# Four heads to a unit for short key ranges, and output projections in halves, in two attentions of a two-block transformer kernel

## The chip, the cores and the metric

One core of a Trainium2 chip runs the whole program. The metric is device time in microseconds (us), the median over several executions. The times of the kernel before are 1931.8, 1932.94 and 1935.67 us, median 1932.94. The engines are called PE (TensorE, matrix products; PEld is its loading of weights), DVE (VectorE), ACT (ScalarE), POOL (GpSimd) and SP (SyncE, which only issues DMAs here).

## What is computed

The reference runs two models after each other on 512 tokens of width 1024, four layers in all, in float32. The change touches the attention of the third and fourth layer only (`fox_attention` with `memory_attention`, and `dilated_attention` with `memory_attention`). Cut to that:

```
h = x                                    # [512, 1024]
for layer in (0, 1):
    xn = rmsnorm(h, norm_mix[layer])
    q, k, v, (f,) qm = split(xn @ w_in)  # 12 heads of 64 for q, k, v; 4 memory heads qm
    if layer == 0:                       # fox: causal, with a forget term per head and key
        sc = q @ k.T / 8 + c[query] - c[key]
    else:                                # dilated: causal, each key weighted by how many
        sc = q @ k.T / 8 + log(count)    # of three dilated windows hold it
    mix = softmax(sc) @ v                # 12 heads, up to 512 keys
    mem_out = softmax(qm @ km.T / 8) @ vm   # 4 heads, 256 memory keys
    h = h + concat(mix, mem_out) @ w_out[layer]
    h = h + conv_ffn(rmsnorm(h, norm_ffn[layer]))
```

(The reference computes the dilated attention as three branches joined by their log-sum-exps; over 512 tokens that is the softmax above, and the kernel uses it in that form.)

## The kernel before

Both attentions come from `attn34` (line 1214), once with `li == 0` (fox) and once with `li == 1` (dilated). It first projects q, k, v and prepares the memory keys, which the change leaves alone. The part that is touched begins at line 1346.

Queries are worked in four blocks of 128 (`qb`), in the order 3, 2, 0, 1. Block `qb` sees `128 * (qb + 1)` keys, so block 3 has 512 and block 0 has 128; the memory heads have 256 keys always. A *unit* is two heads (`j`, 0 to 5 mixing heads, 6 and 7 memory heads) of one query block: 32 units. The loop at line 1424 is a pipeline of three parts on PE. Step `i` issues, in this order:

- **S**, `score` of unit `i` (line 1350): the two heads' products q·k into two PSUM banks, one head in each, and in the fox attention's mixing heads two more matmuls for the forget term. On DVE and ACT the softmax follows: per head one DVE pass that adds the mask and takes the row extreme (line 1372; for memory heads a plain reduction, 1376), one ACT exponential with its sum (1377), then one DVE reciprocal for both heads (1380), and one DVE scaling per head (1382).
- **V**, `value` of unit `i - 2` (line 1396): the products with v, into the bank `o`. After every fourth `j`, `group` (1409) splits the bank into a high part on ACT (`ah`) and a low part on DVE (`al`).
- **T**, `turn_p` of unit `i - 1` (line 1384): transposes of the two heads' probabilities, one PSUM bank a head, each copied out by `evac`, two on ACT to one on DVE.
- whatever is due by `steps.tick()` (1444).

Every S, V and T matmul, and those of the output projection, go through `Chain`, so PE takes them in the order in which they were written. `Steps` holds work to be issued some ticks later. When all eight pairs of a query block are done, `group` books `finish` three ticks later (1417). `finish` (836) does the output projection in four quarters of 256 columns, 24 matmuls each, one quarter a tick (`per=1`), in the bank `misc`, of which there is one; two quarters fill it, and DVE then adds it to `h` (859). After the last quarter come the next layer's norm (`norm_scale`, 237) and, four ticks later, `to_x` (260): eight transposes in two portions that go through `misc` too, each copied out by ACT (268) and DVE (269). These transposes are not in the chain: where they stand in PE's order is set when the program is planned. The last block (`qb` 1) uses `o` for its second half and puts its `to_x` off into the next phase. `finish` is shared with the first layer's attention (882 to 968), which already works with four heads to a unit in the same two score banks and with halves (`per=2`), and two ticks between.

The banks: one `o`, one `misc`, two pairs of score banks `spp`, two `tps` for transposes. The probabilities have four buffers (`p2`), the transposed ones two (`pt`).

Of the kernel before, what the change touches and what calls it, by code (L numbers as in the profile page):

```python
# [8 lines left out]
F32 = mybir.dt.float32  # L9
F32R = mybir.dt.float32r  # L10
BF = mybir.dt.bfloat16
AF = mybir.ActivationFunctionType
OP = mybir.AluOpType
AX = mybir.AxisListType
# [83 lines left out]
def _build(tc, nc, ctx, t, out, dbg, upto):  # L98
    V, A, G, PE = nc.vector, nc.scalar, nc.gpsimd, nc.tensor
# [10 lines left out]
    nrm = pool(ctx, "nrm", 1)  # L110
# [14 lines left out]
    def pst(tag):  # L125
        return banks[tag].tile([128, 512], F32, tag=tag, name=tag)
# [228 lines left out]
    def evac(dst, src):  # L355
        evq[0] += 1
        if evq[0] % 3 == 0:
            V.tensor_copy(dst, src)
        else:
            A.activation(dst, src, AF.Copy)  # L360
# [19 lines left out]
    pp = phase(pst_, "prep", side="right")  # L380
# [6 lines left out]
    qT = l1.tile([128, 4, 512], F32, name="qT")  # L387
    kT = l1.tile([128, 2, 512], F32, name="kT")
    vt = l1.tile([128, 4, 128], F32, name="vt")
# [36 lines left out]
    for tb in range(NB):  # L426
# [7 lines left out]
        tp = pst("ft")  # L434
# [26 lines left out]
    pt = pp.tile([128, 3, 16], F32, name="pt")  # L461
# [288 lines left out]
    steps = Steps()  # L750
# [85 lines left out]
    def finish(steps, ws, cat, tb, gb, x, last, pl, chain=None, per=1):  # L836
        def norm():
            if last:
                norm_block(h[:, tb], gb, x, tb, pl=pl, put_off=pend.append)
            else:  # L840
                norm_block(h[:, tb], gb, x, tb, ("misc", "misc"), pl, lambda f: steps.later(4, f))

        tags = ("misc", "o") if last else ("misc", "misc")
        if chain is None:
            out_proj(ws, cat, tb, tags)
            norm()
            return
        bank = {}

        def quarter(c):  # L850

            half, q = divmod(c, 2)
            if q == 0:
                bank["ps"] = pst(tags[half])
            ps = bank["ps"]
            tm(ps[:, q * 256:(q + 1) * 256], ws[c], cat, pe=chain)
            if q == 1:
                hv = h[:, tb, half * 512:(half + 1) * 512]
                V.tensor_tensor(hv, ps, hv, op=OP.add)
            if c == 3:  # L860
                norm()
            elif (c + 1) % per:
                quarter(c + 1)
            else:
                steps.later(1, lambda: quarter(c + 1))
        quarter(0)
# [11 lines left out]
    steps = Steps()  # L878
    chain = Chain()
# [74 lines left out]
    units = [(qb, kv) for qb in range(NB - 1, -1, -1) for kv in range(2)]  # L954
    sts = {qb: {} for qb in range(NB)}
    for i in range(len(units) + 2):
        if i < len(units):
            qb, kv = units[i]
# [3 lines left out]
        if i > 1:  # L962
            qb, kv = units[i - 2]
# [3 lines left out]
        if 0 < i <= len(units):  # L967
            qb, kv = units[i - 1]
# [14 lines left out]
    qT = l2.tile([128, 8, 512], F32, name="qT2")  # L983
    kT = l2.tile([128, 2, 512], F32, name="kT2")
    vt = l2.tile([128, 4, 256], F32, name="vt2")
# [17 lines left out]
    steps = Steps()  # L1003
# [39 lines left out]
    tp = tps()  # L1043
    for tb in range(NB):
        PE.transpose(tp[:, tb * 8:tb * 8 + 8], wiT[64:72, tb * 128:(tb + 1) * 128], ident[64:72, 64:72])
    V.tensor_scalar(wi.rearrange("p b h -> p (b h)"), tp[:, :32], float(np.float32(8 ** -0.5)), 0.125,
                    op0=OP.mult, op1=OP.mult)
# [9 lines left out]
    for qb in range(1, NB):  # L1057
        n = 128 * (qb + 1)
        qs = slice(qb * 128, qb * 128 + 128)
        s_ = ix.tile([128, 512], F32, tag=f"isc{qb}", name="isc")[:, :n]  # L1060
        for hd in range(8):
            rw = slice((hd % 2) * 64, (hd % 2) * 64 + 64)
# [151 lines left out]
    def attn34(li, x3, w_in, w_out_ap, gain_next):  # L1214
# [132 lines left out]
        steps = Steps()  # L1347
        chain = Chain()

        def score(qb, j, st_):  # L1350
            qs = slice(qb * 128, qb * 128 + 128)
            nm, sm = st_["nm"], st_["sm"]
            m = 128 * (qb + 1) if j < 6 else 256
            rows = [slice(i * 64, i * 64 + 64) for i in range(2)]
            forget = li == 0 and j < 6
            pp = spp()
            for i, rw in enumerate(rows):
                if j < 6:
                    chain.matmul(pp[:, i, :m], qT[rw, j, qs], kT[rw, j, :m], start=True, stop=not forget)
                else:  # L1360
                    chain.matmul(pp[:, i, :m], qmT[rw, j - 6, qs], kmT[rw, j - 6], start=True, stop=True)
            if forget:
                for i in range(2):
                    chain.matmul(pp[:, i, :m], sel[rows[i], 2 * j + i:2 * j + i + 1].to_broadcast([64, 128]),
                                 c24[rows[i], :m], start=False, stop=True)
            h2 = slice(2 * j, 2 * j + 2)
            for i in range(2):
                hd = 2 * j + i
                p2 = ae.tile([128, 512], F32, tag="p2", name="p2", bufs=4)
                src = pp[:, i]  # L1370
                if j < 6:
                    V.tensor_tensor_reduce(out=p2[:, :m], in0=src[:, :m], in1=nlm[:, 512 - m:], scale=1.0,
                                           scalar=3e38, op0=OP.add, op1=OP.min, accum_out=nm[:, hd:hd + 1])
                    src = p2
                else:
                    V.tensor_reduce(nm[:, hd:hd + 1], src[:, :m], axis=AX.X, op=OP.min)
                A.activation(p2[:, :m], src[:, :m], AF.Exp, bias=nm[:, hd:hd + 1], scale=-1.0,
                             accum_out=sm[:, hd:hd + 1])
                st_[hd] = p2
            V.reciprocal(sm[:, h2], sm[:, h2])  # L1380
            for hd in (2 * j, 2 * j + 1):
                V.tensor_scalar(st_[hd][:, :m], st_[hd][:, :m], sm[:, hd:hd + 1], None, op0=OP.mult)

        def turn_p(qb, j, st_):
            m = 128 * (qb + 1) if j < 6 else 256
            st_["pt", j] = []
            for i in range(2):
                p2 = st_[2 * j + i]
                tp = tps()
                for kb in range(m // 128):  # L1390
                    chain.transpose(tp[:, kb * 128:(kb + 1) * 128], p2[:, kb * 128:(kb + 1) * 128], ident)
                pt_ = ae.tile([128, 512], F32, tag="pt", name="pt_", bufs=2)
                evac(pt_[:, :m], tp[:, :m])
                st_["pt", j].append(pt_)

        def value(qb, j, st_):
            m = 128 * (qb + 1) if j < 6 else 256
            jj = j % 4
            if jj == 0:
                st_["po", j // 4] = pst("o")  # L1400
            pov = st_["po", j // 4].rearrange("p (j q) -> p j q", j=4)
            for kb in range(m // 128):
                for i in range(2):
                    hd = 2 * j + i
                    vv = vt[:, kb, hd * 64:(hd + 1) * 64] if j < 6 else vm[:, kb, (hd - 12) * 64:(hd - 11) * 64]
                    chain.matmul(pov[i * 64:(i + 1) * 64, jj], vv, st_["pt", j][i][:, kb * 128:(kb + 1) * 128],
                                 start=kb == 0, stop=kb == m // 128 - 1)

        def group(qb, hg, st_):
            po = st_["po", hg]  # L1410
            ah = ap_.tile([128, 4, 128], F32R, tag="ah", name="ah", bufs=3)
            al = ap_.tile([128, 4, 128], F32R, tag="al", name="al", bufs=3)
            A.activation(f3(ah), po, AF.Copy)
            V.tensor_tensor(f3(al), po, f3(ah).bitcast(F32), op=OP.subtract)
            st_["a", hg] = (ah, al)
            if hg == 1:
                steps.later(3, lambda: finish(
                    steps, wo, lambda k: (st_["a", k // 4][0][:, k % 4], st_["a", k // 4][1][:, k % 4]), qb, gb, xn_,
                    qb == order[-1], ap_ if order.index(qb) % 2 else nrm, chain))

        order = (3, 2, 0, 1)
        units = [(qb, j) for qb in order for j in range(8)]
        sts = {qb: {} for qb in range(NB)}
        for i in range(len(units) + 2):
            if i in (1, 2):
                q = int(i == 2)
                ps = pst("misc")
                fm(ps, w, q * 128, 128, xk(x3))
                A.activation(qmT[:, q], ps, AF.Copy, scale=-0.125)
            if i < len(units):  # L1430
                qb, j = units[i]
                if j == 0:
                    sts[qb]["nm"] = ae.tile([128, 16], F32, tag="nm", name="nm", bufs=2)
                    sts[qb]["sm"] = ae.tile([128, 16], F32, tag="sm", name="sm", bufs=2)
                score(qb, j, sts[qb])
            if i > 1:
                qb, j = units[i - 2]
                value(qb, j, sts[qb])
                if j % 4 == 3:
                    group(qb, j // 4, sts[qb])  # L1440
            if 0 < i <= len(units):
                qb, j = units[i - 1]
                turn_p(qb, j, sts[qb])
            steps.tick()
        steps.drain()
        stx.close()
# [163 lines left out]
```

## Time and profile before

| | us |
|---|---|
| median of 3 runs | 1932.94 |
| the profiled execution, whole | 1937.1 |
| its span, first to last instruction | 1935.2 |
| PE busy | 1833.9 (95%) |
| DVE busy | 1039.4 (54%) |
| ACT busy | 728.6 (38%) |
| stretch of the fox attention from its first memory unit to the last projection | 117.7 |
| the same stretch of the dilated attention | 118.1 |

Busy times come from one execution recorded by the hardware profiler. A matmul's recorded end is modelled and matmuls overlap, so a busy PE need not be a PE at its peak; the granted clock (PEclk, 1.00 is 2.4 GHz and 0.50 is 1.2 GHz) stands beside it. The chain of waits is followed backwards from the last instruction, and each entry is what the end of the program was waiting for at that moment.

### The profile page before, as it was taken

To read this page: it belongs to the slowest core of one execution; us is meant where nothing else is said; L and a number is where in the kernel's file an instruction comes from. 1 tells how busy PE (TensorE), PEld (TensorE's weight loads), DVE (VectorE), ACT (ScalarE), POOL (GpSimd) and SP (SyncE) were. 2 spreads that over 40 slices of the span, in tenths; PEclk is the share of its full clock that TensorE was granted. 3 is DMA by queue.
4 is the path that set the end of the run, shared out by engine and by line. 5 is a ranking of instruction groups with operands and counts; after the bars stand their busy time and mean duration, and the time that the engine had idled before them with its cause. 6 is when DMAs were issued, how large, how long until landed. Compare 5 with 4: busy or idle time off the path is not lost.

```text
span 1935.2 us, 27920 instructions
## 1 busy us (share of the span) xinstructions
PE 1833.9 (95%) x11098; PEld 1540.4 (80%) x11100; DVE 1039.4 (54%) x2199; ACT 728.6 (38%) x1454; POOL 132.9 (7%) x151
## 2 busy tenths in 40 slices
PE   6999969999999999999999999999989899999998
PEld 5987759859789887678888888889957788888886
DVE  5874474268664534664655553366275555555522
ACT  4133353333443334543443341233264444333421
POOL 1332001203120000000000000000000000000000
PEclk9999989969999999989999999999999999999999
DMA  6112321301521432102333322333220043322321
GB/s 207 44 34 88 131 66 51 98 22 56 166 72 41 149 109 77 33 1 66 110 100 88 101 74 98 110 130 98 78 87 1 3 120 98 99 87 82 115 87 66
DMA packets 187898, 161.74 MB, mean 84 GB/s; under 512 B 14568, under 2 KB 170320, under 8 KB 187768
## 3 DMA queue, kind: packets, MB, share of 16 engines
q1 hardware_dynamic: 181168, 144.30, 24.1%
q0 software_dynamic: 2784, 9.00, 1.5%
q10 hardware_dynamic: 3816, 6.66, 1.0%
q8 instruction: 88, 1.44, 0.3%
q14 instruction: 42, 0.34, 0.1%
HBM read 157.88 MB, written 4.74 MB: 84 GB/s over the span
## 4 chain that ended last, share of the span: by engine, by line
PE 81%; DVE 7%; issue 4%; DMA 3%; ACT 3%; POOL 1%; ACTq 0%; POOLq 0%; DVEq 0%; SPq 0%
PE acc L212 19%; PE acc L210 19%; PE acc L211 19%; PE misc L338 6%; PE o L338 3%; PE tps L338 2%; PE spp L338 2%; DVE wl L206 1%; PE sps L1064 1%; PE misc L210 1%; PE misc L211 1%; PE misc L212 1%; PE o L1140 1%; ACT wh L204 1%; DVE xn L247 1%
## 5 line engine op out<-in xcount | busy, mean ns | idle before, releaser
L206 DVE TENSOR_TENSOR wl<-raw,wh 128x1024 fp32r<-128x1024 f32 (+3 forms) x250 | 299.1, 1207 | 408.2 <-ACT wh L204 407.3
L204 ACT ACTIVATE wh<-raw 128x1024 fp32r<-128x1024 f32 (+2 forms) x262 | 270.3, 1044 | 475.6 <-PE acc L211 208.9
L212 PE MATMUL acc<-xh,wl 128*128 128x512 f32 (+2 forms) x1032 | 391.0, 380 | 4.3 <-DVE wl L206 4.3
L210 PE MATMUL acc<-xh,wh 128*128 128x512 f32 (+2 forms) x1032 | 391.6, 381 | 0.7 <-ACT xh L268 0.5
L211 PE MATMUL acc<-xl,wh 128*128 128x512 f32 (+2 forms) x1032 | 391.0, 380 | 0.0
L212 PEld LDWEIGHTS acc<-xh,wl 128*128 128x128 f32 (+1 forms) x1032 | 193.9, 188 | 45.0 <-DVE wl L206 5.9
L210 PE MATMUL acc<-wh,xh 128*128 128x256 f32 (+1 forms) x736 | 224.5, 305 | 3.0 <-ACT xh L268 2.8
L210 PEld LDWEIGHTS acc<-xh,wh 128*128 128x128 f32 (+1 forms) x1032 | 193.1, 188 | 40.7 <-ACT xh L268 1.0
L211 PEld LDWEIGHTS acc<-xl,wh 128*128 128x128 f32 (+1 forms) x1032 | 193.8, 188 | 38.0
L211 PE MATMUL acc<-wl,xh 128*128 128x256 f32 (+1 forms) x736 | 220.6, 300 | 1.1 <-DVE wl L206 1.1
L212 PE MATMUL acc<-wh,xl 128*128 128x256 f32 (+1 forms) x736 | 220.2, 300 | 0.8 <-DVE xl L269 0.8
L210 PEld LDWEIGHTS acc<-wh,xh 128*128 128x128 f32 x736 | 152.5, 207 | 10.1 <-ACT xh L268 5.8
L212 PEld LDWEIGHTS acc<-wh,xl 128*128 128x128 f32 x736 | 152.7, 208 | 6.0 <-issue 4.3
L211 PEld LDWEIGHTS acc<-wl,xh 128*128 128x128 f32 x736 | 152.7, 207 | 4.9 <-issue 3.3
L212 PE MATMUL acc<-wh,gl 128*128 128x512 f32 x352 | 139.2, 395 | 0.0
L210 PE MATMUL acc<-wh,gh 128*128 128x512 f32 x352 | 138.6, 394 | 0.0
L211 PE MATMUL acc<-wl,gh 128*128 128x512 f32 x352 | 138.6, 394 | 0.0
L245 POOL TENSOR_TENSOR rs<-ss,mhalf 128x1 f32<-128x1 f32 x32 | 17.6, 552 | 1479.2 <-DVE ss L243 1470.2
L338 PE MATMUL misc<-wh,ah 128*128 128x256 f32 x280 | 83.0, 296 | 0.0
L338 PE MATMUL misc<-wl,ah 128*128 128x256 f32 x280 | 80.1, 286 | 0.0
L338 PE MATMUL misc<-wh,al 128*128 128x256 f32 x280 | 79.9, 285 | 0.0
L211 PEld LDWEIGHTS acc<-wl,gh 128*128 128x128 f32 x352 | 66.2, 188 | 15.6
(1494 smaller groups left out, 3057.1 us busy)
## 6 DMA issues: line engine op xcount, KB each, us to landing
raw<-in_w_up_dram SPq DMA_DIRECT2D x176, 256.0 KB, 3.1
raw<-in_w_down_dram SPq DMA_DIRECT2D x44, 512.0 KB, 3.6
raw<-in_od_w_in_dram SPq DMA_DIRECT2D x24, 512.0 KB, 3.5
raw<-in_w_in_dil_dram SPq DMA_DIRECT2D x20, 512.0 KB, 3.6
raw<-in_ev_w_in_dram SPq DMA_DIRECT2D x18, 512.0 KB, 4.0
raw<-in_w_out_dram SPq DMA_DIRECT2D x16, 512.0 KB, 3.9
raw<-in_w_in_fox_dram SPq DMA_DIRECT2D x14, 512.0 KB, 4.8
raw<-in_ev_w_out_dram SPq DMA_DIRECT2D x8, 512.0 KB, 4.2
```

The source lines that it names most:

```text
L204: A.activation(hi[:, k0:k1], raw, AF.Copy)
L206: eng.tensor_tensor(lo[:, k0:k1], raw, hi[:, k0:k1].bitcast(F32), op=OP.subtract)
L210: pe.matmul(ps, lh, rh, start=first, stop=False)
L211: pe.matmul(ps, lh, rl, start=False, stop=False)
L212: pe.matmul(ps, ll, rh, start=False, stop=last)
L245: G.tensor_tensor(r, ss[:, 3:4], mhalf[:, :1], op=OP.pow)
L247: V.scalar_tensor_tensor(xn[:, hv[i]], hb[:, hv[i]], r, gb[:, hv[i]], op0=OP.mult, op1=OP.mult)
L338: self.last = op(*a, **k).ins
L1064: PE.matmul(ps[:, :n], qiT[rw, hd // 2, qs], kiT[rw, :n], start=True, stop=True)
L1140: PE.matmul(pov[:, hd % 4], vt[:, kb, kv * 128:(kv + 1) * 128], pt_[:, kb * 128:(kb + 1) * 128], start=kb == 0, stop=kb == qb)
```

## The change

In `attn34`, a unit now holds a tuple of pairs `js`. Blocks with 128 or 256 keys (`qb` 0 and 1) take two pairs, so four heads, to a unit, and so do the memory heads of all blocks. The second pair's scores lie in the same two banks beside the first pair's, and a head's probabilities share a buffer with another's, so that one transposed copy serves two heads. There are 22 units in place of 32. The projection is booked one tick after the last `group` in place of three, which is the tick of the same step, and runs in halves (`per=2`).

```diff
+        def width(qb, js):
+            return 128 * (qb + 1) if js[0] < 6 else 256
...
+        def score(qb, js, st_):
...
+            cols = [slice(a * m, a * m + m) for a in range(len(js))]
             pp = spp()
+            for j, cl_ in zip(js, cols):
+                for i, rw in enumerate(rows):
+                    if j < 6:
+                        chain.matmul(pp[:, i, cl_], qT[rw, j, qs], kT[rw, j, :m], start=True, stop=not forget)
+                    else:
+                        chain.matmul(pp[:, i, cl_], qmT[rw, j - 6, qs], kmT[rw, j - 6], start=True, stop=True)
+                if forget:
+                    for i in range(2):
+                        chain.matmul(pp[:, i, cl_], sel[rows[i], 2 * j + i:2 * j + i + 1].to_broadcast([64, 128]),
+                                     c24[rows[i], :m], start=False, stop=True)
+            ps_ = [ae.tile([128, 512], F32, tag="p2", name="p2", bufs=4) for _ in range(2)]
+            for j, cl_ in zip(js, cols):
                 for i in range(2):
+                    hd = 2 * j + i
+                    p2, src = ps_[i][:, cl_], pp[:, i, cl_]
...
+                    A.activation(p2, src, AF.Exp, bias=nm[:, hd:hd + 1], scale=-1.0, accum_out=sm[:, hd:hd + 1])
+            h2 = slice(2 * js[0], 2 * js[-1] + 2)
             V.reciprocal(sm[:, h2], sm[:, h2])
+            for j, cl_ in zip(js, cols):
+                for i in range(2):
+                    hd = 2 * j + i
+                    V.tensor_scalar(ps_[i][:, cl_], ps_[i][:, cl_], sm[:, hd:hd + 1], None, op0=OP.mult)
+            st_["p", js] = ps_
+
+        def turn_p(qb, js, st_):
+            n = width(qb, js) * len(js)
+            st_["pt", js] = []
+            for p2 in st_["p", js]:
                 tp = tps()
+                for kb in range(n // 128):
                     chain.transpose(tp[:, kb * 128:(kb + 1) * 128], p2[:, kb * 128:(kb + 1) * 128], ident)
                 pt_ = ae.tile([128, 512], F32, tag="pt", name="pt_", bufs=2)
+                evac(pt_[:, :n], tp[:, :n])
...
             if hg == 1:
-                steps.later(3, lambda: finish(
+                steps.later(1, lambda: finish(
                     steps, wo, lambda k: (st_["a", k // 4][0][:, k % 4], st_["a", k // 4][1][:, k % 4]), qb, gb, xn_,
-                    qb == order[-1], ap_ if order.index(qb) % 2 else nrm, chain))
+                    qb == order[-1], ap_ if order.index(qb) % 2 else nrm, chain, 2))
 
         order = (3, 2, 0, 1)
-        units = [(qb, j) for qb in order for j in range(8)]
+        units = [(qb, js) for qb in order
+                 for js in ([(0, 1), (2, 3), (4, 5)] if qb < 2 else [(j,) for j in range(6)]) + [(6, 7)]]
```

`value` takes its transposed probabilities from the shared copies in the same way, and the loop issues S, V, T and the tick in the same order as before.

## Rows read from the trace of the kernel before

**Rows 1.** The page's chain that ended last: share of the span by engine.

```profile
PE 81%; DVE 7%; issue 4%; DMA 3%; ACT 3%; POOL 1%; ACTq 0%; POOLq 0%; DVEq 0%; SPq 0%
```

**Rows 2.** Windows: stretch, us, busy PE, PEld, DVE, ACT, POOL (instructions), PEclk, DMA share, GB/s.

```profile
783.70:901.40 117.70, 108.95 (x901) 88.11 (x900) 65.35 (x220) 51.84 (x169) 1.65 (x3) 0.96 0.01 2
852.70:865.00 12.30, 9.71 (x81) 6.47 (x80) 10.26 (x37) 7.74 (x27) 0.55 (x1) 1.00 0.01 2
1437.90:1556.00 118.10, 108.88 (x865) 86.48 (x864) 64.84 (x220) 52.09 (x170) 1.65 (x3) 0.94 0.01 2
```

**Rows 3.** Chain of waits, fox attention: start us, us, engine, output, line, count.

```profile
805.00 1.02 PE spp L338 x6
806.02 0.81 PE o L338 x12
...
815.96 0.63 PE spp L338 x4
...
842.93 0.48 PE spp L338 x6
843.41 0.37 PE o L338 x4
...
868.07 0.75 PE spp L338 x6
868.82 0.59 PE o L338 x8
869.40 0.59 PE tps L338 x4
```

**Rows 4.** The same, dilated attention.

```profile
1457.40 0.85 PE spp L338 x4
...
1491.33 0.42 PE spp L338 x4
```

**Rows 5.** The same, first layer's attention, units of four heads with half projections.

```profile
277.97 1.06 PE spp L338 x8
279.03 1.02 PE o L338 x16
...
281.08 5.72 PE misc L338 x48
286.80 0.65 PE spp L338 x8
```

**Rows 6.** Chain of waits, first layer's attention, its last two projections.

```profile
304.31 5.67 PE misc L338 x48
...
316.08 6.91 PE misc L338 x48
...
330.65 0.49 PE misc L266 x4
331.14 1.54 PE o L338 x13
```

**Rows 7.** Groups by line, 783 to 902 us: count | busy us, mean ns | idle, releaser.

```profile
L338 PE MATMUL tps<-ident,p 128*128 128x128 f32 x119 | 19.9, 293 | 2.8 <-DVE p L1382 2.8
...
L1382 DVE TENSOR_SCALAR p<-p,sm 128x256 f32<-128x256 f32 x28 | 8.6, 350 | 0.4
L1377 ACT ACTIVATE p<-spp,nm 128x256 f32<-128x256 f32 x16 | 7.5, 469 | 9.5 <-DVE nm L1376 9.4
...
L1376 DVE TENSOR_REDUCE nm<-spp 128x1 f32<-128x256 f32 x16 | 6.7, 420 | 6.3 <-PE spp L338 3.8 <-ACT p L1377 2.5
...
L1414 DVE TENSOR_TENSOR al<-o,ah 128x512 fp32r<-128x512 f32 x8 | 5.5, 685 | 1.9 <-ACT ah L1413 1.9
...
L1413 ACT ACTIVATE ah<-o 128x512 fp32r<-128x512 f32 x8 | 4.7, 586 | 3.3 <-PE o L338 3.3
...
L1377 ACT ACTIVATION_READ_ACCUMULATOR p<-spp,nm 128x1 f32 x16 | 3.1, 197 | 0.0
```

**Rows 8.** Window in the fox attention with a lower clock, columns as in Rows 2.

```profile
827.30:837.50 10.20, 10.20 (x58) 7.87 (x59) 6.05 (x29) 4.86 (x19) 0.00 (x0) 0.50 0.00 0
```

More of the change, by code (lines that the diff above doesn't have):

```diff
@@ L1348, in attn34 @@
         chain = Chain()
-        def score(qb, j, st_):
+        def width(qb, js):
+            return 128 * (qb + 1) if js[0] < 6 else 256
+        def score(qb, js, st_):
             qs = slice(qb * 128, qb * 128 + 128)
             nm, sm = st_["nm"], st_["sm"]
-            m = 128 * (qb + 1) if j < 6 else 256
+            m = width(qb, js)
             rows = [slice(i * 64, i * 64 + 64) for i in range(2)]
-            forget = li == 0 and j < 6
+            forget = li == 0 and js[0] < 6
+            cols = [slice(a * m, a * m + m) for a in range(len(js))]
@@ L1356, in score @@
             pp = spp()
[L1357 to L1362, printed above, removed]
-                for i in range(2):
-                    chain.matmul(pp[:, i, :m], sel[rows[i], 2 * j + i:2 * j + i + 1].to_broadcast([64, 128]),
-                                 c24[rows[i], :m], start=False, stop=True)
@@ L1366, in score @@
[L1366 to L1379, printed above, removed]
@@ L1380, in score @@
-            V.reciprocal(sm[:, h2], sm[:, h2])
[L1381 to L1388, printed above, removed]
+            for j, cl_ in zip(js, cols):
[8 more added lines that the diff above has]
+                                     c24[rows[i], :m], start=False, stop=True)
@@ new lines, in score @@
+            ps_ = [ae.tile([128, 512], F32, tag="p2", name="p2", bufs=4) for _ in range(2)]
+            for j, cl_ in zip(js, cols):
+                for i in range(2):
+                    hd = 2 * j + i
+                    p2, src = ps_[i][:, cl_], pp[:, i, cl_]
+                    if j < 6:
+                        V.tensor_tensor_reduce(out=p2, in0=src, in1=nlm[:, 512 - m:], scale=1.0,
+                                               scalar=3e38, op0=OP.add, op1=OP.min, accum_out=nm[:, hd:hd + 1])
+                        src = p2
+                    else:
+                        V.tensor_reduce(nm[:, hd:hd + 1], src, axis=AX.X, op=OP.min)
+                    A.activation(p2, src, AF.Exp, bias=nm[:, hd:hd + 1], scale=-1.0, accum_out=sm[:, hd:hd + 1])
@@ L1389, in turn_p @@
+            h2 = slice(2 * js[0], 2 * js[-1] + 2)
+            V.reciprocal(sm[:, h2], sm[:, h2])
+            for j, cl_ in zip(js, cols):
[7 more added lines that the diff above has]
+            for p2 in st_["p", js]:
                 tp = tps()
-                for kb in range(m // 128):
+                for kb in range(n // 128):
@@ L1391, in turn_p @@
                     chain.transpose(tp[:, kb * 128:(kb + 1) * 128], p2[:, kb * 128:(kb + 1) * 128], ident)
                 pt_ = ae.tile([128, 512], F32, tag="pt", name="pt_", bufs=2)
[L1393 to L1407, printed above, removed]
+                evac(pt_[:, :n], tp[:, :n])
@@ new lines, in turn_p, with value @@
+                st_["pt", js].append(pt_)
+        def value(qb, js, st_):
+            nk = width(qb, js) // 128
+            if js[0] % 4 == 0:
+                st_["po", js[0] // 4] = pst("o")
+            pov = st_["po", js[0] // 4].rearrange("p (j q) -> p j q", j=4)
+            for a, j in enumerate(js):
+                for kb in range(nk):
+                    for i in range(2):
+                        hd = 2 * j + i
+                        vv = vt[:, kb, hd * 64:(hd + 1) * 64] if j < 6 else vm[:, kb, (hd - 12) * 64:(hd - 11) * 64]
+                        ks = slice((a * nk + kb) * 128, (a * nk + kb + 1) * 128)
+                        chain.matmul(pov[i * 64:(i + 1) * 64, j % 4], vv, st_["pt", js][i][:, ks],
+                                     start=kb == 0, stop=kb == nk - 1)
@@ L1430, in attn34 @@
             if i < len(units):
-                qb, j = units[i]
-                if j == 0:
+                qb, js = units[i]
+                if js[0] == 0:
                     sts[qb]["nm"] = ae.tile([128, 16], F32, tag="nm", name="nm", bufs=2)
                     sts[qb]["sm"] = ae.tile([128, 16], F32, tag="sm", name="sm", bufs=2)
-                score(qb, j, sts[qb])
+                score(qb, js, sts[qb])
             if i > 1:
[L1437 to L1440, printed above, removed]
+                qb, js = units[i - 2]
+                value(qb, js, sts[qb])
+                if js[-1] % 4 == 3:
+                    group(qb, js[-1] // 4, sts[qb])
             if 0 < i <= len(units):
-                qb, j = units[i - 1]
-                turn_p(qb, j, sts[qb])
+                qb, js = units[i - 1]
+                turn_p(qb, js, sts[qb])
             steps.tick()
```

## The prediction

> **What bounds the kernel now.** First the page's chain that ended last: PE makes up 81% of it, DVE 7% and ACT 3% [rows 1]. So only time taken off PE's own sequence, or a wait of PE, is worth anything. Then the windows, cut to the two stretches which the change reaches, from the first memory unit of query block 3 to the end of the last projection: 117.7 us (fox) and 118.1 us (dilated) [rows 2]. PE is recorded busy for 109 us of each, but PEld for only 88 and 86, and the clock is 0.96 and 0.94 there. To see what PE could do without waits, I read the chain of waits in order of time where it names nothing but PE, one step after another, and take each piece's length from it [rows 3 to 5].
>
> The pieces, at full clock: S of a pair costs 0.48, 0.75 and 1.02 us for 128, 256 and 384 keys in fox, 0.63 for a memory pair [rows 3], and 0.42 and 0.85 for 128 and 384 keys in the dilated attention [rows 4], where 256 keys cost what a memory pair does, 0.63. V costs 0.37, 0.59 and 0.81 for 4, 8 and 12 matmuls, and T of the same unit costs the same as V (0.59 and 0.59) [rows 3]. V of 16 is 1.02, and a half projection 5.72, so a quarter is 2.86 [rows 5].
>
> PE's work in the fox stretch before: S 8 x 0.63 + 6 x 1.02 + 6 x 0.48 + 6 x 0.75 = 18.5. V: two units of block 3 at 1.02, then 6 x 0.81, 6 x 0.37, 6 x 0.59 and 8 memory units x 0.59 = 17.4. T: the same with one unit of block 3 = 16.4. Sixteen quarters 45.8. Three `to_x` inside the stretch, each two portions near 0.5 [rows 6], 3.3 with their starts. Sum 101.4, so PE waits or runs slow for 117.7 - 101.4 = 16.3 us. Dilated: S is 8 x 0.63 + 6 x 0.85 + 6 x 0.42 + 6 x 0.63 = 16.4, the rest is equal: 99.3, and 18.8 us of waits.
>
> In steps that hold a projection PE never waits, since all of ACT's and DVE's work lies beside it. The waits lie between: in one such stretch DVE is busy 10.26 of 12.3 us [rows 2], and PE's transposes wait for the scaled probabilities, 2.8 us [rows 7]. Its four steps hold S 4 x 0.75, V and T 8 x 0.59 and a `to_x` of 1.1, 8.8 us, so 3.5 us of that stretch are waits.
>
> **What the change takes from PE's work.** The matmuls stay, number and shape. But a piece has a fixed part: V goes 0.37, 0.59, 0.81, 1.02 for 4, 8, 12, 16 matmuls, which is 0.15 us and 0.055 a matmul [rows 3, 5]. Two pieces merged pay it once. The four-head units measured in the first layer show it for S: 1.06 at 256 keys against 2 x 0.63, and 0.65 at 128 against 2 x 0.42 [rows 4, 5].
>
> After, fox: S 4 x 1.06 (memory) + 6 x 1.02 + 3 x s0 + 3 x s1. The trace has no four-head S with a forget term. Two pairs unmerged are the upper end, 0.96 and 1.50; the first layer's value plus twice the pairs' difference between fox and dilated is the lower, 0.77 and 1.30. I take 0.9 and 1.4, the middle: S 17.3. V: 2 x 1.02 + 6 x 0.81 + 3 x 0.59 + 3 x 1.02 + 4 x 1.02 = 15.8; T 14.8; projections 45.8; `to_x` 3.3. Sum 97.0, 4.4 less. Dilated: S 4 x 1.06 + 6 x 0.85 + 3 x 0.65 + 3 x 1.06 = 14.5, sum 94.2, 5.1 less. Together **9.5 us** off PE's work; 7 to 11 by the ends of s0 and s1 and of the fixed part (0.15 to 0.21).
>
> On ACT and DVE ten copies and ten reciprocals an attention go away. They count only where PE waits for them, so they are in the next part.
>
> **What becomes of the waits.** Renumber the steps of the changed loop: unit 6 is block 3's memory unit, 7 to 12 and 13 block 2, 14 to 17 block 0, 18 to 21 block 1. Halves fall in steps 8 and 9, 15 and 16, 19 and 20, and after step 23. Uncovered are 7, 10 to 14, 17 and 18, and 21 to 23. For one attention:
>
> (a) T behind a memory unit. Its softmax is a reduction 0.42, four exponentials one behind the other at 0.57 (0.47 alone, 0.67 with the whole read of its sum, and the read overlaps in part), and a scaling of 0.35 for each of three heads before the first transpose can go, with two hand-overs and the reciprocal 0.3: 0.42 + 2.28 + 1.05 + 0.3 = 4.05 [rows 7]. PE's cover is V, T, S, V of the steps between: near 4.1 at unit 6, 3.3 at 13, 3.2 at 17, and V, T, V = 3.1 at 21, where no S follows. Waits 0 + 0.7 + 0.9 + 1.0 = 2.6.
> (b) Steps 10 to 14: five in a row with `norm` and `to_x` of block 3 in them. By the stretch above (3.5 in four steps) up to 4.4; PE has more of its own here (0.81 against 0.59 a piece), I take 3.0.
> (c) Steps 17, 18 and 21, 22 carry DVE's norm of blocks 2 and 0: half the stretch above each, and a little more as the norm's part does not halve: 2.0 + 2.0.
> (d) Step 23: V of the last unit waits for its own copies with nothing between: 1.0. None of this was so before: a pair's copy is half as long.
> (e) Step 20. `to_x` of block 2 comes due together with the second half of block 0 and is written before it, and both want the one `misc` bank. The first layer shows that order: from the end of its half at 309.98 to the next half at 316.08 go 6.1 us, through the add to `h` and two portions with their copies [rows 6]. Here S, V and T of step 20 (1.4 + 1.02 + 1.02) and the transposes (1.1) fill 4.5 of it: 1.6. I take 2.0. Ends: 0 if the planner moves these transposes ahead of the first half, 4.1 if it lets only V run beside.
> (f) The projection right behind `group`. `ah` and `al` take 0.59 + 0.69 [rows 7]; T (at least 0.8) and the twelve matmuls on the first four heads (a quarter of a half's 48, 1.4 us) run meanwhile. Three times 0.3 for a busy ACT, about 1.0.
> (g) Lower clock. Fox had one stretch of 10.2 us at 0.50 [rows 8], of which PE lost up to half. It followed a wait of PE for a norm. I count 1.5 to 3, take 2.2.
>
> Sum: 2.6 + 3.0 + 4.0 + 1.0 + 2.0 + 1.0 + 2.2 = 15.8, against 16.3 and 18.8 before. That gives back 0.5 and 3.0, **3.5 us**. `to_x` of block 0, which before stood in front of the last projection, now falls inside its second half, which uses bank `o`; the first layer shows such transposes in the midst of a half with no wait [rows 6].
>
> Nothing moves on SP or POOL but POOL's small power in the norm, which goes with it. The next phase's first weights wait for the same half as before.
>
> **Sum.** 9.5 + 3.5 = 13.0 us off the profiled execution of 1937.1, whose span is 1935.2: 1924.1. That execution lies 4.2 above the median of the runs, 1932.94. The same 13.0 off the median gives 1919.9, and I say 1920.
>
> **A rule that speaks against it.** The trace shows DVE at 83% in an uncovered stretch and PE waiting for its scalings [rows 2, 7]. The Trainium skill, Perfetto Trace Analysis, section Optimizing Scalar/DVE Operations, says that where these engines cause bubbles on others without being saturated, breaking instructions up may let work finish sooner, and that grouping pays where they are saturated; here the change groups. By that rule it would come out as in the slower rival below. At 83% the row is nearer to the second half of the sentence.
>
> **Rivals.**
> *The longer softmax (slower).* A unit of four heads gives PE nothing until four exponentials have run, and what stands on DVE before it (a norm's 1.5, an `al` 0.7) is added. Place: the uncovered T's and the two T's in the steps after a four-head S of blocks 0 and 1, six an attention. Price: up to 2.2 us each, 13 an attention, 26 in all, against 13 gained: 1932.9 + 13 = 1946. It decides from 1.1 us each. For it: DVE's 83%. Against: a pair's work is spared on DVE too (ten reciprocals, ten copies), and a four-head unit of the first layer, once a projection lies in its step, runs without a wait [rows 5].
> *The one projection bank (small gain).* In (e) the two copies to the next layer's input queue behind the exponentials of a four-head unit, 2.3 us each: 2 + 4.6 an attention, 9.2 more in all. 13.0 - 9.2 = 3.8, 1929. For it: the first layer's order [rows 6], where the clock was lower afterwards (the next half took 6.91). Against: the planner may order the copies ahead.
> *Waits mostly gone (larger gain).* If the planner fills the uncovered steps as well as the first layer's, waits fall to about 8 an attention: 9.5 + 8.3 + 10.8 = 28.6, 1904. Against: nine uncovered steps stay.
>
> **How the numbers follow.** My forecast, a gain of 8 to 20, has 0.45; the small gain (0 to 8) 0.25; the larger gain 0.15; the slower rival 0.15. What a measurement of this kernel can tell from no change is about 0.2%, 3.9 us. The forecast and the larger gain are faster (0.60), of the small gain half (0.12); the other half and a little of the slower rival are the same (0.15); slower 0.13. The range, 1907 to 1936, holds the forecast and the small gain whole, two thirds of the larger gain and the mildest of the slower one.
>
> **What would show it.** Steps with a half should run S + V + T + 5.72 without a wait: 8.3 us for block 2, near 9.2 for block 1 in fox. The two stretches should end 5 and 8 us shorter. Wrong if: T of four-head units waits over 1.1 us in most uncovered steps; a second half starts over 8 us after the first one's end in step 20; or merged S, V, T take as long as two pairs, in which case the 9.5 us fall away.

## The result, and the profile after

The changed kernel takes 1957.64 us (median of 4 runs, 1954.83 to 1958.82), the kernel before 1932.71: ratio 1.0127, 95% interval 1.0112 to 1.0142. That is 25 us slower, where 1920 us and a gain were forecast. The profiled executions lie 17.7 apart (1954.8 and 1937.1; of the two kernels the one was below its median and the other above), and those 17.7 us are what the rows can explain.

The page's chain that ended last, share of the span by engine:

```profile
PE 78%; DVE 8%; ACT 5%; issue 4%; DMA 4%; POOL 1%; SPq 0%; POOLq 0%; DVEq 0%; ACTq 0%
```

PE's share falls by three points against [rows 1], ACT's rises by two and DVE's by one: more of the end now waits on the softmax. Windows over the same stretches as [rows 2], and over two steps behind memory units (columns as there):

```profile
783.10:910.30 127.20, 106.97 (x903) 90.44 (x902) 62.76 (x205) 51.78 (x158) 1.65 (x3) 0.92 0.01 2
846.40:861.80 15.40, 10.85 (x84) 7.97 (x84) 10.18 (x37) 8.16 (x27) 0.55 (x1) 0.78 0.00 1
884.50:897.70 13.20, 9.15 (x73) 6.72 (x72) 6.48 (x15) 5.26 (x14) 0.55 (x1) 0.74 0.00 0
1445.80:1572.50 126.70, 106.76 (x866) 89.17 (x866) 62.45 (x205) 51.81 (x158) 1.65 (x3) 0.89 0.02 6
```

The stretches went from 117.7 to 127.2 and from 118.1 to 126.7 us, 18.1 together: all of the difference is inside them. DVE and ACT are less busy or as busy as before, and yet the clock fell from 0.96 to 0.92 and from 0.94 to 0.89. The chain in order of time, block 0, a step with a half under four-head units; it answers to the 128-key rows of [rows 3]:

```profile
838.76 0.82 PE spp L338 x12
839.58 0.59 PE o L338 x8
840.16 0.59 PE tps L338 x4
840.75 5.74 PE misc L338 x48
```

S of four heads costs 0.82 where two pairs cost 0.96, V and T 0.59 each where they cost 0.74. So PE's own work did shrink as forecast, and such a step has no wait. Who made PE wait in the fox stretch (total us, times, longest):

```profile
PE tps L338 <- DVE p L1389: 8.9, 4, 2.9
PE o L338 <- DVE al L1422: 3.9, 3, 1.8
PE misc L266 <- DVE xl L269: 2.5, 1, 2.5
PE misc L338 <- DVE xl L269: 1.4, 1, 1.4
...
PE misc L338 <- DVE al L1422: 1.1, 2, 0.9
```

Before, T waited 2.8 us for scaled probabilities [rows 7]; now 8.9, four times, and the four are the four memory units (1.5, 2.4, 2.9 and 2.1 us). In the dilated attention the view from 1445 to 1573 us has this line; 10.6 of it in four waits are the memory units, the fifth lies ahead of the stretch:

```profile
PE tps L338 <- DVE p L1389: 11.6, 5, 3.0
```

Here is the last memory unit of fox, first on DVE, then on ACT (start, us, engine, line, what; in brackets the idle time before it and who ended it):

```profile
887.02 1.41 DVE L247 SCALAR_TENSOR_TENSOR xn<-h,rs,gb 128x512 f32<-128x512 f32 x2 [0.73 <-POOL rs L245]
888.35 0.42 DVE L1382 TENSOR_REDUCE nm<-spp 128x1 f32<-128x256 f32 x1
888.69 0.68 DVE L1422 TENSOR_TENSOR al<-o,ah 128x512 fp32r<-128x512 f32 x1
889.40 0.43 DVE L1382 TENSOR_REDUCE nm<-spp 128x1 f32<-128x256 f32 x1
890.46 0.42 DVE L1382 TENSOR_REDUCE nm<-spp 128x1 f32<-128x256 f32 x1 [0.63 <-ACT p L1383]
891.51 0.42 DVE L1382 TENSOR_REDUCE nm<-spp 128x1 f32<-128x256 f32 x1 [0.63 <-ACT p L1383]
892.57 0.18 DVE L1385 RECIPROCAL sm<-sm 128x4 f32<-128x4 f32 x1 [0.63 <-ACT p L1383]
```

```profile
888.80 0.47 ACT L1383 ACTIVATE p<-spp,nm 128x256 f32<-128x256 f32 x1 [0.82 <-DVE nm L1382]
...
889.86 0.47 ACT L1383 ACTIVATE p<-spp,nm 128x256 f32<-128x256 f32 x1
...
890.92 0.47 ACT L1383 ACTIVATE p<-spp,nm 128x256 f32<-128x256 f32 x1 [0.49 <-DVE nm L1382]
...
891.97 0.47 ACT L1383 ACTIVATE p<-spp,nm 128x256 f32<-128x256 f32 x1 [0.49 <-DVE nm L1382]
```

Read the two side by side. A memory head's reduction (DVE) and its exponential (ACT) both read the score tile in PSUM, and the next head's reduction starts only when the exponential before it has ended. DVE waits 0.63 for ACT, then ACT waits 0.49 for DVE: 1.05 us a head, 4.2 for four, in which each engine is idle for about half of the time. A mixing head's DVE pass writes its scores to SBUF and the exponential reads there, and those heads do not take turns: in block 1 the four passes of a unit run without a gap from 870.55 to 872.0 us, while the exponentials have begun at 871.01.

The Trainium skill, PSUM — Partial Sum Buffer, section PSUM bank collisions raise a hardware error, says that no two engines may access one bank and quadrant at once, reads included, and that semaphores should guard by bank and quadrant, or more simply by bank. The trace agrees in so far as the two do not read together in these lines, but the turns here go over the whole two-bank tile: the reduction at 890.46 reads the first bank and waits for an exponential that reads the second. By the order of the heads in the code all three turns are between different banks; no run tried a guard by bank.

### The profile page after: what moved, and what is told of

The parts are those of the page before. It is cut to its first block, busy times and chain, and to the rows that moved or that the text cites. A ratio compares the mean times of both kernels' runs of the same rounds, so it can differ in the third digit from the quotient of the medians.

```text
span 1953.0 us, 27793 instructions
## 1 busy us (share of the span) xinstructions
PE 1825.1 (93%) x11098; PEld 1541.0 (79%) x11100; DVE 1033.4 (53%) x2166; ACT 727.4 (37%) x1427; POOL 132.9 (7%) x151
## 4 chain that ended last, share of the span: by engine, by line
PE 78%; DVE 8%; ACT 5%; issue 4%; DMA 4%; POOL 1%; SPq 0%; POOLq 0%; DVEq 0%; ACTq 0%
PE acc L212 19%; PE acc L210 19%; PE acc L211 19%; PE misc L338 6%; PE o L338 2%; ACT p L1383 2%; PE tps L338 2%; PE spp L338 1%; DVE wl L206 1%; PE sps L1064 1%; PE misc L210 1%; PE misc L211 1%; PE misc L212 1%; DVE xn L247 1%; PE o L1140 1%
## 5 line engine op out<-in xcount | busy, mean ns | idle before, releaser
L241 ACT ACTIVATE xn<-h 128x512 f32<-128x512 f32 x48 | 30.3, 631 | 155.3 <-DVE h L859 109.7
```

Source lines behind the costliest of these rows:

```text
L241: A.activation(xn[:, hv[i]], hb[:, hv[i]], AF.Square, accum_out=ss[:, i:i + 1])
```

## Experiments

All are compared with the kernel before on the same chip; differences between experiments go by the ratios, with 0.001 as 1.9 us. Where a stretch is given, it is as in the windows above, fox and dilated. `put` is the number of ticks from a norm to its transposes (4 in the kernel before); a line `...` marks what is left out of a cut.

**Four heads with quarters.** Projections in quarters from the same step; the transposes of block 2 at tick 5.

```diff
...
-    qb == order[-1], ap_ if order.index(qb) % 2 else nrm, chain, 2))
+    qb == order[-1], ap_ if order.index(qb) % 2 else nrm, chain, put=5 if qb == 2 else 4))
```

> The units of the changed kernel (four heads for short key ranges and memory), but projections in quarters from the same step on, one a step; the norm's transposes of query block 2 come one tick later. Theory A (a memory unit's softmax is long, because its reductions on DVE and exponentials on ACT take turns, and PE waits for it in steps without a projection): quarters lie under the memory units of blocks 2 and 0 (units 17 and 21), so two of four long waits go, some 5 us an attention: 1942 to 1948 us. Theory B (halves bunch the projections and leave steps uncovered, whatever the units are): nearly all of the loss goes, 1930 to 1938 us.

Ratio 1.0006 (0.9993 to 1.0020), 1936.33 us. Some 23 of the 25 us come back, which is theory B's figure and twice theory A's; but quarters lie under two of the four memory units too, so alone this does not decide. For the other two, which still stand in steps without a projection, T goes on waiting: 2.7 us in fox, 5.8 in the dilated attention.

**Halves alone.** The kernel before, with:

```diff
-                steps.later(3, lambda: finish(
+                steps.later(1, lambda: finish(
...
-                    qb == order[-1], ap_ if order.index(qb) % 2 else nrm, chain))
+                    qb == order[-1], ap_ if order.index(qb) % 2 else nrm, chain, 2))
```

> The kernel before with units of two heads, but projections in halves, booked for the same step. Theory A: no long softmax, so within 5 us of the kernel before, 1928 to 1938 us. Theory B: the loss is here: 1945 to 1958 us.

Ratio 0.9991 (0.9976 to 1.0005), 1933.78 us: no difference from before. With units of pairs, and the memory heads' reductions as they are, bunching the projections costs nothing; theory B, by which the loss would be here, falls.

**Memory heads from SBUF.** The changed kernel, with:

```diff
+        zero = ae.tile([128, 1], F32, name="zero")
+        V.memset(zero, 0.0)
...
-                        V.tensor_reduce(nm[:, hd:hd + 1], src, axis=AX.X, op=OP.min)
+                    V.tensor_tensor_reduce(out=p2, in0=src, in1=nlm[:, 512 - m:] if j < 6 else zero.to_broadcast([128, 256]), scale=1.0,
+                                           scalar=3e38, op0=OP.add, op1=OP.min, accum_out=nm[:, hd:hd + 1])
+                    src = p2
```

> The changed kernel, but the memory heads' scores go through the same DVE pass as the others (adding a zero), which writes them to SBUF, and the exponentials read there, so that DVE and ACT no longer take turns on the score tile. Theory A: in the trace a head takes 1.05 us of alternation against 0.57 for an exponential, 1.9 us a memory unit, eight units: 10 to 15 us less than the changed kernel, 1943 to 1948 us, and T behind memory units waits 1 us less or more each. Theory B: within 4 us of the changed kernel, 1954 to 1960 us.

Ratio 1.0017 (1.0001 to 1.0033), 1939.14 us: some 21 of 25 us come back by the ratios, more than the 10 to 15 expected. The same unit on DVE (columns as above):

```profile
881.24 1.42 DVE L247 SCALAR_TENSOR_TENSOR xn<-h,rs,gb 128x512 f32<-128x512 f32 x2 [0.73 <-POOL rs L245]
882.57 0.42 DVE L1378 CUSTOM_DVE_ANT_0 p<-spp,zero 128x256 f32<-128x256 f32 x1
...
882.91 0.42 DVE L1378 CUSTOM_DVE_ANT_0 p<-spp,zero 128x256 f32<-128x256 f32 x1
...
883.25 0.42 DVE L1378 CUSTOM_DVE_ANT_0 p<-spp,zero 128x256 f32<-128x256 f32 x1
...
883.60 0.42 DVE L1378 CUSTOM_DVE_ANT_0 p<-spp,zero 128x256 f32<-128x256 f32 x1
...
883.94 0.69 DVE L1420 TENSOR_TENSOR al<-o,ah 128x512 fp32r<-128x512 f32 x1
885.14 0.18 DVE L1383 RECIPROCAL sm<-sm 128x4 f32<-128x4 f32 x1 [0.51 <-ACT p L1381]
```

From the first pass to the reciprocal 2.6 us instead of 4.2. PE's waits in its fox stretch:

```profile
PE o L338 <- DVE al L1420: 6.0, 3, 2.8
...
PE tps L338 <- DVE p L1387: 0.3, 1, 0.3
```

T's wait fell from 8.9 to 0.3. Part of it moved: V now waits 6.0 us for the split of the `o` bank, 3.9 in the changed kernel. The two together fell from 12.8 to 6.3. What is left stands mostly at the memory units of blocks 0 and 1 (2.4 and 2.8 us), where the lines above show on DVE a norm's scaling (`xn`) and the four passes ahead of the split (`al`): no turns, but work in front.

**Memory heads in pairs.** The changed kernel, with:

```diff
-                 for js in ([(0, 1), (2, 3), (4, 5)] if qb < 2 else [(j,) for j in range(6)]) + [(6, 7)]]
+                 for js in ([(0, 1), (2, 3), (4, 5)] if qb < 2 else [(j,) for j in range(6)]) + [(6,), (7,)]]
```

> The changed kernel, but memory heads in units of two as before (26 units); blocks 0 and 1 keep four heads. Theory A: a memory unit takes two turns in place of four, so most of the waits behind it go: 1938 to 1948 us. Theory B: the halves stay, and two more uncovered steps a block: 1953 to 1962 us.

Ratio 0.9962 (0.9948 to 0.9976), 1928.53 us, lower than either theory said and 0.4% under the kernel before. PE's waits in its fox attention, from 783 us on:

```profile
PE misc L338 <- DVE xl L269: 3.5, 1, 3.5
PE o L338 <- DVE al L1422: 2.8, 3, 1.0
PE tps L338 <- DVE p L1389: 1.9, 4, 0.5
```

T waits 1.9 in all, and the `misc` bank is now the longest wait. From the second experiment this one differs only by the four-head units of blocks 0 and 1: they gain 0.0029, some 6 us, with intervals that just meet; the prediction's pieces of PE's work give 5.4 for these blocks.

**Both: pairs, from SBUF.** The two edits above together.

> Memory heads in units of two, and read from SBUF as in the third experiment; blocks 0 and 1 four heads, halves. Theory A (taking turns makes the memory softmax late, in pairs too, if less): the pairs lose one turn each, 0.5 us in up to 16 units, so 3 to 7 us under the fourth experiment's ratio: 0.993 of the kernel before. Theory C (only the length of a four-head unit counts, pairs are covered anyway): the same as the fourth experiment, 0.996.

Ratio 0.9941 (0.9918 to 0.9965), 1926.32 us. Its interval overlaps the fourth's, so this does not show that turns cost pairs anything. Against the third it shows something else. The two differ only in whether a memory unit holds four heads or two, neither has turns, and they lie 0.0076 apart, some 15 us, with intervals that do not meet. So a four-head memory unit costs time without turns too. Part of the reason is V's wait for the split, 6.0 us in the fox attention of the third and 2.6 here; how much of the 15 us it explains stays open.

**The kernel before, memory heads from SBUF.** The same replacement of the reduction, in the kernel before.

> The kernel before, with nothing but the memory heads read from SBUF. Theory A: pairs take turns too (one turn in place of three), and 16 memory units stand in uncovered and covered steps alike: 0 to 6 us faster than the kernel before. Theory C: no change, within 3 us.

Ratio 0.9957 (0.9937 to 0.9977), 1928.76 us: 8 us, a little more than theory A's upper end. So the kernel before seems to have paid for turns already, but its one trace shows only part of it: the fox stretch takes 113.1 us at a clock of 1.00 (117.7 at 0.96 before), the dilated one 119.1 (118.1); T waits 2.8 us in fox as before, its longest wait 0.9 in place of 1.6.

**Reductions first.** The changed kernel; for memory units the exponentials are written in a loop of their own behind the four reductions, and still read PSUM:

```diff
-                    A.activation(p2, src, AF.Exp, bias=nm[:, hd:hd + 1], scale=-1.0, accum_out=sm[:, hd:hd + 1])
+                    if j < 6:
+                        A.activation(p2, src, AF.Exp, bias=nm[:, hd:hd + 1], scale=-1.0, accum_out=sm[:, hd:hd + 1])
+            if js[0] == 6:
+                for j, cl_ in zip(js, cols):
+                    for i in range(2):
+                        hd = 2 * j + i
+                        A.activation(ps_[i][:, cl_], pp[:, i, cl_], AF.Exp, bias=nm[:, hd:hd + 1], scale=-1.0,
+                                     accum_out=sm[:, hd:hd + 1])
```

> The changed kernel, but of a memory unit all four reductions are written ahead of the four exponentials, which still read PSUM. If taking turns is the cause (theory A), the chain 4 x 1.05 = 4.2 us becomes 4 x 0.34 and 4 x 0.57 = 3.6 us and DVE no longer stands between: a third to a half of what the third experiment gave, 6 to 10 us below the changed kernel: 1946 to 1951 us. If instead it is that the exponentials read PSUM at all (theory D), nothing: 1953 to 1959 us.

Ratio 1.0048 (1.0032 to 1.0064), 1945.12 us. By the ratios 15 us below the changed kernel, more than the 6 to 10 expected: over half of the loss for an order of writing. On DVE:

```profile
882.27 1.41 DVE L1382 TENSOR_REDUCE nm<-spp 128x1 f32<-128x256 f32 x4
883.60 0.68 DVE L1429 TENSOR_TENSOR al<-o,ah 128x512 fp32r<-128x512 f32 x1
885.68 0.18 DVE L1392 RECIPROCAL sm<-sm 128x4 f32<-128x4 f32 x1 [1.40 <-ACT p L1389]
```

Four reductions in one go, 3.4 us to the reciprocal, and T waits 2.1 us in fox. By theory D nothing would have come back, so it falls as the main cost; taking turns is that. The 0.0031 by which this run lies above the third (the intervals just overlap) are not explained.

**Bank order.** As the fifth, with the transposes of block 2 at tick 3 and of block 0 at tick 5 (`put={3: 4, 2: 3, 0: 5, 1: 4}[qb]`).

> As the first of this set, and the norm's transposes of block 2 come one tick earlier, those of block 0 one later, so that none falls right before a half projection in the one misc bank. The first half of block 0 waited 3.5 us for that bank in the fox attention of the fourth experiment. If that wait is on the path, 3 to 6 us less than the first of this set over both attentions; if the planner only moves it elsewhere, within 2 us.

Ratio 0.9926 (0.9905 to 0.9946), 1923.36 us. 3 us under the fifth, the lower end of what was expected, but the intervals overlap: a gain over the fifth is likely, not shown. Windows of its two stretches:

```profile
783.30:892.70 109.40, 102.00 (x902) 85.26 (x902) 63.19 (x228) 52.16 (x164) 1.65 (x3) 1.00 0.01 2
1430.50:1539.30 108.80, 102.20 (x868) 84.06 (x867) 61.76 (x227) 51.23 (x162) 1.65 (x3) 0.98 0.01 2
```

18 us shorter each than in the changed kernel, at a clock of 1.00 and 0.98.

**Norm later.** The changed kernel; the norm is issued one step after the projection, its transposes three ticks on (`steps.later(1, norm)`, `put=3`).

> The changed kernel, but the norm after a projection is issued one step later, behind the softmax of the next unit on DVE and ACT, and its transposes with it at tick 3 after that. Theory E (besides taking turns, what stands on DVE ahead of a memory unit's softmax, the add and the norm, 2.3 us with its waits, makes T wait): T of units 17 and 21 waits some 2 us less each, and the transposes of block 2 no longer fall between the two halves of block 0: 5 to 10 us below the changed kernel, ratio 1.008 to 1.010. Theory A alone: the turns set the wait, within 4 us, ratio 1.011 to 1.014.

Ratio 1.0099 (1.0061 to 1.0137). The interval reaches from theory E to theory A, and the trace says why it decides little: the planner still put the norm's scaling among the memory unit's reductions (chain, in order of time).

```profile
846.28 0.75 DVE xn L247
847.03 0.33 DVE nm L1384
...
847.69 0.60 DVE al L1424
848.29 0.33 DVE nm L1384
848.62 0.66 DVE xn L247
849.28 0.41 DVE nm L1384
```

How much of the wait is due to work that stands ahead on DVE stays open by this run.

**Pairs everywhere, from SBUF.** The fifth without four-head units: `[(j,) for j in range(6)]` for all blocks.

> Halves, all units in pairs, memory heads read from SBUF: the fifth experiment without the four-head units of blocks 0 and 1. If merging spares PE fixed time and its steps are covered, as the fourth and fifth experiments suggest, this is slower than the fifth: six merges an attention at 0.5 us, 6 us over both, ratio 0.997. If the four-head units of blocks 0 and 1 gain nothing, 0.994 as there.

Ratio 0.9996 (0.9979 to 1.0012), 1932.41 us, against 0.9941 for the fifth. The four-head units of blocks 0 and 1 are worth some 10 us here; 6 were expected, and 6 is what the fourth and the second give. Two more comparisons bear on what was said above. The sixth has the same units from SBUF but quarters, booked two steps later, and stands at 0.9957, with an interval that just does not meet this one: here the halves cost some 8 us, which the second experiment does not show. And the second, with halves and pairs but reductions from PSUM, stands at 0.9991: under halves reading from SBUF gains pairs nothing. So how projections and softmax interlock decides what either is worth, and the 8 us of the sixth do not carry over.

**Bank order and norm later.** The eighth with the norm issued one step later, as in the ninth, and `put={3: 3, 2: 2, 0: 4, 1: 4}[qb]`.

> The eighth experiment (pairs of memory heads from SBUF, four heads in blocks 0 and 1, halves, bank order) with the norm one step later. With memory pairs read from SBUF the softmax is short, so the norm ahead of it should count less than in the ninth: 0 to 3 us below the eighth, ratio 0.991 to 0.993; if the norm's delay makes the transposes late instead, 0.993 to 0.995.

Ratio 0.9935 (0.9916 to 0.9955), 1922.14 us: the same as the eighth, within the intervals. These two are the fastest versions run, some 0.7% under the kernel before.

## Why the prediction was wrong

**PE's work (9.5 us): right.** With the measured S of 0.82 and, for 256 keys, 1.30 in fox (868.8 to 870.1 us), PE's work is 96.4 and 94.2 us, 10 in all less than before. A step with a half under block 2 takes 8.4 us without a wait (801.56 to 809.92), forecast 8.3. The fourth and the tenth experiment show that the merge in blocks 0 and 1 is worth having.

**Step (a), T behind a memory unit: the one that failed.** I gave its softmax 4.05 us: one reduction, four exponentials one behind the other, three scalings and the hand-overs. In the trace the first transpose starts behind the first scaling, so like for like I had 3.35. Measured from the first reduction to that transpose are 4.9 us at the unit shown above (888.35 to 893.28) and 5.4 to 6.1 at the other three of fox, into whose chain work of other units is mixed. The difference at the unit shown is the turns: four reductions and four exponentials alternate, 4.2 us to the reciprocal, where I had added up 2.7 and the hand-overs. T's waits were forecast at 2.6 us an attention and measured at 8.9 in fox and 10.6 in the dilated attention, 1.5 to 3.0 us each, all over the 1.1 that I had named as the mark. Removing the turns took them to 0.3 in fox and the time from 1.0127 to 1.0017, and changing their order alone took it to 1.0048. The sign was in my own rows and I read past it: the reduction's row [rows 7] says that 2.5 us of DVE's idle time before reductions ended with `ACT p`, an exponential. In a pair that is one turn; four heads make three of it. I read that row for its length only.

**Step (c), the norm on DVE: right in kind, low in size.** The memory units of blocks 0 and 1 also start late: from the end of S to the first reduction go 2.7 us, against 1.1 in blocks 3 and 2, because the add to `h` and the norm stand ahead on DVE. V's wait for `al` and T's wait at these two units come to 4.3 and 3.9 us, where (a) and (c) together had 5.9 for both. Without turns 2.7 and 2.8 are left (third experiment). So the turns are the largest single cause, not the only one: merging the memory heads costs some 32 us in the changed kernel (1.0127 against 0.9962 in the fourth), and still some 15 where no turns are taken (third against fifth). And it takes the halves to make it cost so much: with quarters beside two of the four memory units, the first experiment is level with the kernel before.

**Steps (b) and (d): high.** Steps 10 to 14, T of the memory unit aside, have waits of 1.2 and 0.8 us, forecast 3.0; the last unit's V waits 0.1, forecast 1.0.

**Step (g), the clock: low in size.** With the waits came more time at the lower clock. Its four windows in the fox stretch of the changed kernel (columns as in [rows 2]):

```profile
829.20:832.60 3.40, 3.40 (x30) 2.95 (x31) 1.89 (x12) 1.91 (x10) 0.00 (x0) 0.51 0.00 0
853.10:859.90 6.80, 4.28 (x20) 3.17 (x20) 3.63 (x15) 3.46 (x12) 0.00 (x0) 0.50 0.00 0
877.00:880.40 3.40, 3.21 (x15) 3.21 (x16) 0.14 (x1) 0.00 (x0) 0.00 (x0) 0.51 0.02 5
890.70:897.50 6.80, 4.54 (x27) 3.27 (x25) 2.62 (x8) 1.73 (x5) 0.00 (x0) 0.50 0.00 0
```

The first came 1.4 us after T's wait for block 2's memory unit (2.4 us), the second during the wait for block 0's (2.9), the third at the end of the waits for the `misc` bank (2.5 and 1.4), the fourth 1.2 us after V's wait for `al` (1.8) and before T's for block 1's (2.1). They make 20.4 us at half the full clock, against 10.2 before [rows 8]. PE is busy for 15.4 of them, so up to 7.7 us are lost, where 10.2 had cost up to 5.1 and I counted 2.2. In the eighth experiment, with short waits, the stretches are at 1.00 and 0.98. That the waits lower the clock fits all of this; no run changed one without the other.

**Step (e), the one bank: right in kind, low in size.** The chain between block 0's halves:

```profile
868.94 0.70 DVE h L859
...
871.01 2.09 ACT p L1383 x8
...
873.33 1.14 DVE p L1389 x4
...
875.13 0.67 PE misc L266 x4
...
877.19 7.44 PE misc L338 x48
```

From the first half's end at 868.91 to the next half's start at 877.19 go 8.3 us, where [rows 6] showed 6.1 and I went by that: a four-head softmax (2.09 and 1.14) stands between on ACT and DVE. PE waited 2.5 + 1.4 us there, forecast 2.0. It was over the 8 us that I had named as the mark; in the dilated attention it was 8.7.

**Step (f): right**, 1.1 us measured for 1.0.

**The rivals.** The longer softmax was the right direction at 0.15. Its price of 2.2 us a wait holds for memory units (8.9 in four). Its reason was a long softmax with work ahead of it on DVE. That is there, 2.7 us at two units of four, but the reason left out the turns, which the runs show to be the larger part. It also laid two of the six waits on blocks 0 and 1, where four-head units are a gain. The rival of the one projection bank came true as a wait (3.9 and 4.1 us), but not as the outcome. As for the Trainium skill's rule on breaking instructions up, which the prediction cites: in the changed kernel's stretch 884.5 to 897.7, DVE is busy 6.48 of 13.2 us, not 83%, and there the half of the rule for engines that are not saturated is the one that applied. For the mixing heads of blocks 0 and 1 it did not.

**Adding up.** Waits and lost clock in fox: 127.2 - 96.4 = 30.8 us, against 16.3 before and 15.8 forecast; dilated 32.5, against 18.8 and 15.8. In fox the listed waits are 20.1 of it and the clock up to 7.7; some 3 us are in no row.

## What to carry to other kernels

Before merging units, follow one unit's chain through every engine and write down each hand-over, not only each duration: an idle time "ended by" the other engine on a small group is the sign of two engines taking turns, and it grows with each head that is put behind. Where a pass over PSUM must be made anyway, try letting it write to SBUF and the next engine read there: of the runs above that differ by this alone, the third gained 21 us on the changed kernel, the sixth 8 on the kernel before, the fifth 4 on the fourth (within the intervals), and the tenth nothing on the second. A merge that spares fixed costs should be tried on each kind of unit by itself: here it was worth 6 to 10 us in one kind and cost 15 to 32 in the other. And a change to the order of the projections should be tried with each of these, since halves were free beside one kind of unit and dear beside another.

## What the runs showed that I had not expected

That the mask pass with its full output costs no more than a plain reduction of the same size: 0.42 us each at 128x256, and in either kind the next starts 0.34 us after the last. So the SBUF copy of the memory scores was free on DVE. The kernel before ran 8 us faster with it; with halves and pairs it gained nothing (0.9996 against 0.9991).
